# A two-layer hybrid model on one core: the order, one sum and one turning around the half-wide chunk of the gated FFN

## The chip, the cores and the metric

The kernel runs on one core of one Trainium2 chip. The metric is the device time of one execution in microseconds, as the median of several runs. All numbers are float32; the matrix products take float32 values split into a high part in the "fp32r" format and a low part.

## The reference, cut to what matters

Two layers, each with an FFN, a mixer, a cross attention and a second FFN. The change lies in the FFN, which is called four times. `x` is 256 tokens by 1024, the hidden width `D_FF` is 2816.

```python
def swiglu(x, w_gate, w_up, w_down):
    return (jax.nn.silu(x @ w_gate) * (x @ w_up)) @ w_down
...
for l in range(DEPTH):
    h = layer_norm(ALPHA * h + 0.5 * swiglu(h, ffn1_gate[l], ffn1_up[l], ffn1_down[l]),
                   ln_g[l, 0], ln_b[l, 0])
    ...
    h = layer_norm(ALPHA * h + 0.5 * swiglu(h, ffn2_gate[l], ffn2_up[l], ffn2_down[l]),
                   ln_g[l, 3], ln_b[l, 3])
```

## The kernel before

**Products in three parts.** Every weight tile is loaded by a DMA into a `raw` buffer and split (`split`, L74): ScalarE casts it to the high part `whi` (L75), VectorE subtracts that from it for the low part `wlo` (L76). `mm_rows` (L153) then issues three products on TensorE for each pair: high by high, high by low, low by high. All matrix products pass line L129. There are six `raw` buffers and eight of each half, of 128 by 1024 (`bufs` at L86, L106, L107).

**Chunks of the hidden width.** `ffn` (L420) goes through 2816 hidden columns in five chunks of 512 and one, the sixth, of 256, the half-wide chunk. For each it makes the gate's and the up projection's products, applies `silu` and the multiplication, turns the result so that hidden columns lie on partitions (`turn`, L464: four DMAs into the tile `dealt`, two VectorE transposes into `square`, a split into `ah` and `al`), and later multiplies it with two slabs of the down projection (`slab` L732, `both` L756), which add up in four banks called `dn`. Slab (c, u) is the half u of chunk c.

**Chunks by seven.** Some chunks (`sevens`, L738) are computed by `by_seven` (L595), with seven block products for a 2 by 2 block product in place of eight: tokens are halved (tile 0 and 1), the inner width is halved, and gate and up take the place of the two column blocks. The weight sums that this needs are made in place, in the raw tiles: `w00` begins as the gate's first half, `w01` as the up projection's first half, `w10` as the gate's second half, `w11` as the up projection's second half. `parts_of(r, plus)` (L628) first adds `plus` to `r` by VectorE (L632) where it is given, and then splits `r`. `more` (L666) adds a block of a matrix to a raw tile by an adding transfer, a DMA that GpSimd issues (L668). The sums of the tokens' blocks, `bx`, are made once per FFN and held in `kTh` and `kTl`. A `run` (L645) is twelve products into one bank of `o`; `taken` (L663) copies a bank into a tile by ScalarE (L664), and `put` (L650) combines a bank with a tile by VectorE (L651). `o[0]` is used by four runs, of which the second to the fourth go on adding to what the first left: between them `taken` copies the bank's state into `s`, `e` and `f`. For the half-wide chunk those tiles are parts of one called `both`.

In the first FFN of the first layer chunks 2 and 4 go by seven (counted from 0). In the three others chunks 2, 4 and 5 do, so the half-wide chunk 5 is computed by seven three times.

**The order around the half-wide chunk.** In the program's order it runs: `o[0]` with `w00`; `o[1]` with `bx[0]` and `w00` plus `w01`; `o[2]` with `w10`; the first half of the products of slab (3,0) (`between[0]`, the list given at L774, half of them because `steps` is `(0,)`); `o[0]` with `bx[1]` and `w00` plus `w11`; then, since `steps` at L690 is reversed for this chunk, `o[3]` with `bx[3]` and `w11`; `o[0]` with `bx[2]` and `w01`; `o[0]` with `part_of_x(1, 1)` and `w00` plus `w10`. `left` (L695) then does the activation, the multiplication (L698) and the turning. Behind that come the other half of slab (3,0), slab (3,1), and in `ending` (L806) slabs (4,0), (4,1) and (5,0).

**What sets the order of execution.** The program is not executed in the order in which it is written. Within each engine a scheduler of the framework, when the program is built, sets the order: it runs its own estimate of every instruction and takes, whenever an engine is free, the first instruction in the program's order that it believes ready. On the chip each engine then works in that fixed order and waits by semaphores. `tc.issue_after(ins)` queues what its block emits for the engine of `ins` behind `ins`; instructions for other engines are not held. `lows[-1]` is the last emitted VectorE subtraction of a split. The DMA issues stand in the queues of SyncE (SP), ScalarE and GpSimd (POOL).

Of the kernel before, what the change touches and what calls it, by code (L numbers as in the profile page):

```python
# [8 lines left out]
F32 = mybir.dt.float32  # L9
# [8 lines left out]
P = 128  # L18
# [4 lines left out]
NT = SEQ // P  # L23
# [5 lines left out]
CHUNK = 512  # L29
# [31 lines left out]
def model(ctx: ExitStack, tc: tile.TileContext, t: dict, out: bass.AP):  # L61
    nc = tc.nc
# [9 lines left out]
    loads, normed, lows, turns = [], [], [], []  # L72

    def split(hi, lo, src):  # L74
        nc.scalar.copy(hi, src)  # L75
        lows.append(nc.vector.tensor_tensor(lo, src, hi.bitcast(F32), op=ALU.subtract))  # L76
# [343 lines left out]
    def ffn(l, name, n, pend=None, last=False, early=None):  # L420
        gate, up, down = (t[f"{name}_{x}"][l] for x in ("gate", "up", "down"))
        with tc.tile_pool(name="ffn", bufs=2, reuse_waits="tile") as fp:
            acts = []

            def act_tiles():
                ah = fp.tile([P, 4, SEQ], F32R, tag="ah", name="ah", bufs=3)
                al = fp.tile([P, 4, SEQ], F32R, tag="al", name="al", bufs=3)
                return ah, al
# [33 lines left out]


            def turn(s):  # L464
                ah, al = act_tiles()
                n = s.shape[2] // P
                x = fp.tile([P, 4, NT, P], F32, tag="dealt", name="dealt", bufs=1)[:, :, :, 0 : 32 * n]
                for a in range(4):
                    (nc.scalar if n < 4 and a % 2 else nc.sync).dma_start(x[a * 32 : a * 32 + 32], s[:, :, a * 32 * n : (a + 1) * 32 * n])
                d = fp.tile([P, NT, 4, P], F32, tag="up", name="square", bufs=1)[:, :, 0:n, :]  # L470
                for i in range(NT):
                    nc.vector.transpose(
                        d[:, i].rearrange("p k (b r) -> p b k r", b=4),
                        x[:, :, i, :].rearrange("p b (k j) -> p b k j", k=n),
                    )
                d = d.rearrange("p i k t -> p k i t")
                split(*(y[:, 0:n].rearrange("p k (i t) -> p k i t", i=NT) for y in (ah, al)), d)
                return ah, al

            def first():  # L480

# [113 lines left out]
            def by_seven(c0, ncol, bx, between):  # L595
# [76 lines left out]
                taken(s[:, 0, :], o[0])  # L672
                run(o[1], bx[0], parts_of(w00, w01))
                more(w01, up, 1)
                run(o[2], part_of_x(0, 1), parts_of(w10))
                between[0]()
                put(s[:, 0, :], o[2], ALU.add, s[:, 0, :])
                w11 = block(up, 1, pieces(*homes[2]))
                run(o[0], bx[1], parts_of(w00, w11), True)
                if ncol == CHUNK:  # L680
                    more(w00, gate, 1)
                taken(e, o[0])
# [4 lines left out]
                    lambda: (run(o[0], bx[2], parts_of(w01), True), taken(f, o[0])),  # L687
                    lambda: (o.append(bank()), run(o[3], bx[3], parts_of(w11))),
                ]
                for step in steps if ncol == CHUNK else steps[::-1]:  # L690
                    step()
                put(f, o[1], ALU.subtract, f)
                run(o[0], part_of_x(1, 1), parts_of(w00, None if ncol == CHUNK else w10), True)
# [46 lines left out]
            bx = []  # L740
# [24 lines left out]
            later = (0, 0, 0, 2, 0, 2) if early is None else (0, 1, 0, 1, 0, 2)  # L765
            for c, (c0, ncol) in enumerate(chunks):
                if not c:
                    acts.append(first())
                    ys = [[acc((P, 512), "dn") for _ in range(2)] for _ in range(NT)]
                elif c in sevens:  # L770
                    half = []
                    left = by_seven(
                        c0, ncol, bx,
                        [lambda: both(*todo.pop(0))] * 2 if ncol == CHUNK else  # L774
                        [lambda: (half.append(slab(3, 0)), both(3, 0, half[0], (0,))), lambda: None],
                    )
                else:
                    acts.append(hidden(c0) if ncol == CHUNK else last_hidden(c0, turn_memory))
                if c == 1 and early is None:
                    bx.extend(blocks_of_x())  # L780
                if c == 5:
# [8 lines left out]
                    nc.gpsimd.tensor_copy(early_memory[:, 0:2048:256], acts[2][0][:, 0, 0:8].bitcast(F32))  # L790
                    turn_memory = load_memory(fp, loads[-1])
                if c in sevens:
                    acts.append(left())
                    if ncol < CHUNK:
                        both(3, 0, half[0], (1,))
                        both(3, 1)
                else:
                    for _ in range(later[c]):
                        both(*todo.pop(0))
# [539 lines left out]
```

## Time and profile before

| | us |
|---|---|
| median of 3 runs | 1067.16 |
| lowest and highest | 1066.97, 1067.39 |
| the profiled execution | 1066.68 |
| its span, first to last instruction | 1065.0 |
| TensorE busy within the span | 1052.1 |
| VectorE busy within the span | 933.6 |
| ScalarE busy within the span | 661.5 |

The granted TensorE clock of the profiled execution is 0.998 of full speed. The profile is that of one execution. PE is TensorE, DVE VectorE, ACT ScalarE, POOL GpSimd and SP SyncE; L129 is line 129 of the kernel. A row of the timeline gives the start in us from the span's start, the duration, engine, line and operation, output and inputs, the number of instructions merged, and in brackets the engine's idle time before it and what ended that. A matrix product's duration in the timeline is longer than its distance to the next, since they overlap; the distance is what it costs.

### The profile page before, as it was taken

The page shows a single profiled execution, that of the slowest core. Times are in us where ns is not written, and L with a number is a line of the kernel's source. Part 1 is how long each engine was busy: PE and PEld are TensorE (multiplying, and loading weights), DVE is VectorE, ACT ScalarE, POOL GpSimd, SP SyncE. Part 2 cuts the span into 40 slices and gives each one's busy share as a digit, 9 for nine tenths or more (in the row PEclk, how much of TensorE's full clock was granted, in tenths as well). Part 3 has the DMA queues.
Part 4 walks back from the last instruction along what each step waited for, and adds up shares of the span by engine and source line. Part 5 has one row for each costly group of instructions (what it writes and reads, how often), then busy time and mean ns, then how long its engine had stood idle before and what let it go on. Part 6 is the DMA issues. An engine that isn't in the chain of part 4 may idle for free.

```text
span 1065.0 us, 16506 instructions
## 1 busy us (share of the span) xinstructions
PE 1052.1 (99%) x6014; PEld 934.7 (88%) x6014; DVE 933.6 (88%) x1246; ACT 661.5 (62%) x909; POOL 90.9 (9%) x122
## 2 busy tenths in 40 slices
PE   9999999999999999999999999999999999999997
PEld 7888888989899888889888888888998998888886
DVE  6998898989988789888998987989899788898787
ACT  6675775676557466655665755666774655675661
POOL 8002001000000001010001001010000000000000
PEclk9999999999999999999999999999999999999999
DMA  9999984754675589987788987866636665899862
GB/s 363 294 310 289 261 273 158 250 168 153 215 270 183 166 279 234 356 193 223 246 298 232 315 259 208 270 219 223 204 118 221 238 232 176 240 300 298 236 185 76
DMA packets 143745, 251.06 MB, mean 236 GB/s; under 512 B 12784, under 2 KB 53520, under 8 KB 143664
## 3 DMA queue, kind: packets, MB, share of 16 engines
q1 hardware_dynamic: 130656, 228.89, 64.1%
q0 software_dynamic: 10800, 19.55, 10.7%
q10 hardware_dynamic: 2208, 1.57, 0.5%
q8 instruction: 47, 0.77, 0.3%
q14 instruction: 34, 0.28, 0.1%
HBM read 234.50 MB, written 1.05 MB: 221 GB/s over the span
## 4 chain that ended last, share of the span: by engine, by line
PE 92%; DVE 4%; ACT 2%; issue 1%; DMA 1%; ACTq 0%; DVEq 0%
PE acc L129 60%; PE dn L129 29%; DVE wlo L76 2%; ACT whi L75 1%; PE acc L196 1%; DVE raw L632 1%; PE dn L1024 0%; DMA lng<-in_ln_g_dram 0%; DMA h<-in_x_dram 0%; DVE halves L651 0%; PE dn L1098 0%; DVE sg L698 0%; PE acc L512 0%; PE dn L1097 0%; PE dn L1086 0%
## 5 line engine op out<-in xcount | busy, mean ns | idle before, releaser
L75 ACT CAST whi<-raw 128x1024 fp32r<-128x1024 f32 (+1 forms) x453 | 456.4, 1042 | 202.6 <-PE dn L129 60.9
L76 DVE TENSOR_TENSOR wlo<-raw,whi 128x1024 fp32r<-128x1024 f32 (+1 forms) x453 | 534.2, 1208 | 52.5 <-ACT whi L75 47.9
L129 PE MATMUL acc<-whi,xT 128*128 128x512 f32 (+1 forms) x1064 | 314.0, 373 | 3.4 <-ACT both L664 3.4
L129 PEld LDWEIGHTS acc<-whi,xT 128*128 128x128 f32 x1064 | 199.1, 189 | 31.2 <-ACT both L664 4.6
L129 PE MATMUL acc<-wlo,xT 128*128 128x512 f32 (+1 forms) x532 | 197.9, 372 | 0.0
L129 PE MATMUL dn<-whi,ah 128*128 128x512 f32 x346 | 131.5, 380 | 0.0
L129 PE MATMUL dn<-wlo,ah 128*128 128x512 f32 x346 | 131.1, 379 | 0.0
L129 PE MATMUL dn<-whi,al 128*128 128x512 f32 x346 | 131.1, 379 | 0.0
L129 PE MATMUL acc<-xT,whi 128*128 128x512 f32 x480 | 117.8, 382 | 0.2
L129 PEld LDWEIGHTS acc<-wlo,xT 128*128 128x128 f32 x532 | 100.6, 189 | 13.2
L129 PEld LDWEIGHTS acc<-xT,whi 128*128 128x128 f32 x480 | 86.6, 190 | 10.5 <-ACT whi L75 0.7
L129 PE MATMUL dn<-whi,xT 128*128 128x512 f32 x288 | 87.8, 381 | 0.0
L129 PEld LDWEIGHTS dn<-whi,al 128*128 128x128 f32 x346 | 65.4, 189 | 9.3
L129 PEld LDWEIGHTS dn<-whi,ah 128*128 128x128 f32 x346 | 65.4, 189 | 9.0
L129 PEld LDWEIGHTS dn<-wlo,ah 128*128 128x128 f32 x346 | 65.4, 189 | 8.9
L129 PEld LDWEIGHTS acc<-xT,wlo 128*128 128x128 f32 x480 | 62.9, 191 | 3.2
L129 PE MATMUL acc<-xT,wlo 128*128 128x256 f32 x480 | 63.3, 275 | 0.0
L129 PE MATMUL acc<-wlo,kTh 128*128 128x512 f32 (+1 forms) x176 | 61.7, 351 | 0.0
L129 PE MATMUL acc<-whi,kTl 128*128 128x512 f32 (+1 forms) x176 | 61.7, 351 | 0.0
L129 PE MATMUL acc<-whi,kTh 128*128 128x512 f32 (+1 forms) x176 | 61.7, 351 | 0.0
L129 PEld LDWEIGHTS dn<-whi,xT 128*128 128x128 f32 x288 | 54.4, 189 | 7.6 <-DVE xT L76 0.2
L129 PE MATMUL dn<-wlo,xT 128*128 128x512 f32 x144 | 54.6, 379 | 0.0
(245 smaller groups left out, 1288.6 us busy)
## 6 DMA issues: line engine op xcount, KB each, us to landing
raw<-in_ffn_up_dram SPq DMA_DIRECT2D x88, 512.0 KB, 5.7
raw<-in_ffn_down_dram SPq DMA_DIRECT2D x88, 512.0 KB, 6.1
raw<-in_ffn_gate_dram SPq DMA_DIRECT2D x84, 512.0 KB, 5.4
raw<-in_w_in_dram SPq DMA_DIRECT2D x48, 512.0 KB, 4.8
dealt<-sg SPq DMA_DIRECT2D x80, 128.0 KB, 4.9
raw<-in_ffn_up_dram POOLq DMA_DIRECT2D x19, 512.0 KB, 6.0
raw<-in_ffn_gate_dram POOLq DMA_DIRECT2D x16, 512.0 KB, 10.1
raw<-in_ca_k_dram SPq DMA_DIRECT2D x16, 512.0 KB, 5.3
```

What stands on the lines that cost most here:

```text
L75: nc.scalar.copy(hi, src)
L76: lows.append(nc.vector.tensor_tensor(lo, src, hi.bitcast(F32), op=ALU.subtract))
L129: nc.tensor.matmul(o, w, x, start=start, stop=stop, skip_group_check=more)
L196: turns.append(nc.tensor.transpose(pt[:, k, :], src[:, (4 * j + k) * P : (4 * j + k + 1) * P], unit))
L632: nc.vector.tensor_tensor(r[i], r[i], plus[i], op=ALU.add)
```

## The change

Three edits, all of which take effect only where chunk 5 goes by seven.

1. The products of the first half of slab (3,0) come after the run of `o[0]` with `bx[1]` (they move from `between[0]` to `between[1]`), and the runs with `bx[2]` and `bx[3]` go in the order in which they are listed, as in the wide chunks. So each of the uses of `o[0]` from the second on has other products ahead of it.
2. `w00`, holding gate's first half plus up's first half at that point, gets up's second half by a second adding transfer. It was added from `w11` by VectorE.
3. `turn` now gives back a function with its second part (the transposes and the split). For chunk 4 that part is emitted after the whole of `by_seven` of chunk 5, with VectorE's share queued behind the last subtraction of it; everywhere else it is called at once.

```diff
--- before.py
+++ after.py
@@ -462,20 +462,25 @@
 
 
             def turn(s):
-                ah, al = act_tiles()
                 n = s.shape[2] // P
                 x = fp.tile([P, 4, NT, P], F32, tag="dealt", name="dealt", bufs=1)[:, :, :, 0 : 32 * n]
                 for a in range(4):
-                    (nc.scalar if n < 4 and a % 2 else nc.sync).dma_start(x[a * 32 : a * 32 + 32], s[:, :, a * 32 * n : (a + 1) * 32 * n])
-                d = fp.tile([P, NT, 4, P], F32, tag="up", name="square", bufs=1)[:, :, 0:n, :]
-                for i in range(NT):
-                    nc.vector.transpose(
-                        d[:, i].rearrange("p k (b r) -> p b k r", b=4),
-                        x[:, :, i, :].rearrange("p b (k j) -> p b k j", k=n),
-                    )
-                d = d.rearrange("p i k t -> p k i t")
-                split(*(y[:, 0:n].rearrange("p k (i t) -> p k i t", i=NT) for y in (ah, al)), d)
-                return ah, al
+                    queue = nc.scalar if n < 4 and a % 2 else nc.sync
+                    queue.dma_start(x[a * 32 : a * 32 + 32], s[:, :, a * 32 * n : (a + 1) * 32 * n])
+
+                def rest():
+                    ah, al = act_tiles()
+                    d = fp.tile([P, NT, 4, P], F32, tag="up", name="square", bufs=1)[:, :, 0:n, :]
+                    for i in range(NT):
+                        nc.vector.transpose(
+                            d[:, i].rearrange("p k (b r) -> p b k r", b=4),
+                            x[:, :, i, :].rearrange("p b (k j) -> p b k j", k=n),
+                        )
+                    d = d.rearrange("p i k t -> p k i t")
+                    split(*(y[:, 0:n].rearrange("p k (i t) -> p k i t", i=NT) for y in (ah, al)), d)
+                    return ah, al
+
+                return rest
 
             def first():
 
@@ -672,11 +677,13 @@
                 taken(s[:, 0, :], o[0])
                 run(o[1], bx[0], parts_of(w00, w01))
                 more(w01, up, 1)
+                if ncol < CHUNK:
+                    more(w00, up, 1)
                 run(o[2], part_of_x(0, 1), parts_of(w10))
                 between[0]()
                 put(s[:, 0, :], o[2], ALU.add, s[:, 0, :])
                 w11 = block(up, 1, pieces(*homes[2]))
-                run(o[0], bx[1], parts_of(w00, w11), True)
+                run(o[0], bx[1], parts_of(w00, w11 if ncol == CHUNK else None), True)
                 if ncol == CHUNK:
                     more(w00, gate, 1)
                 taken(e, o[0])
@@ -687,7 +694,7 @@
                     lambda: (run(o[0], bx[2], parts_of(w01), True), taken(f, o[0])),
                     lambda: (o.append(bank()), run(o[3], bx[3], parts_of(w11))),
                 ]
-                for step in steps if ncol == CHUNK else steps[::-1]:
+                for step in steps:
                     step()
                 put(f, o[1], ALU.subtract, f)
                 run(o[0], part_of_x(1, 1), parts_of(w00, None if ncol == CHUNK else w10), True)
@@ -765,17 +772,17 @@
             later = (0, 0, 0, 2, 0, 2) if early is None else (0, 1, 0, 1, 0, 2)
             for c, (c0, ncol) in enumerate(chunks):
                 if not c:
-                    acts.append(first())
+                    acts.append(first()())
                     ys = [[acc((P, 512), "dn") for _ in range(2)] for _ in range(NT)]
                 elif c in sevens:
                     half = []
                     left = by_seven(
                         c0, ncol, bx,
                         [lambda: both(*todo.pop(0))] * 2 if ncol == CHUNK else
-                        [lambda: (half.append(slab(3, 0)), both(3, 0, half[0], (0,))), lambda: None],
+                        [lambda: None, lambda: (half.append(slab(3, 0)), both(3, 0, half[0], (0,)))],
                     )
                 else:
-                    acts.append(hidden(c0) if ncol == CHUNK else last_hidden(c0, turn_memory))
+                    acts.append(hidden(c0)() if ncol == CHUNK else last_hidden(c0, turn_memory))
                 if c == 1 and early is None:
                     bx.extend(blocks_of_x())
                 if c == 5:
@@ -790,7 +797,10 @@
                     nc.gpsimd.tensor_copy(early_memory[:, 0:2048:256], acts[2][0][:, 0, 0:8].bitcast(F32))
                     turn_memory = load_memory(fp, loads[-1])
                 if c in sevens:
-                    acts.append(left())
+                    if ncol < CHUNK:
+                        with tc.issue_after(lows[-1].ins):
+                            acts[4] = acts[4]()
+                    acts.append(left() if c + 1 in sevens else left()())
                     if ncol < CHUNK:
                         both(3, 0, half[0], (1,))
                         both(3, 1)
```

## The prediction

> **What bounds the kernel now.** I read the page first: where the span lies, and how much of it each engine works.
>
> ```profile
> span 1065.0 us, 16506 instructions
> ...
> PE 1052.1 (99%) x6014; PEld 934.7 (88%) x6014; DVE 933.6 (88%) x1246; ACT 661.5 (62%) x909; POOL 90.9 (9%) x122
> ```
>
> TensorE (PE) works 1052.1 of 1065.0 us. The change adds and removes no matrix product, so it can gain only what PE stands idle, and it loses whatever new idle time it makes. The view of waits, for PE alone, has three rows:
>
> ```profile
> PE acc L129 <- ACT both L664: 3.4, 3, 1.2
> PE dn L493 <- DVE kTh L488: 1.5, 1, 1.5
> PE acc L512 <- DMA h<-in_x_dram: 0.6, 1, 0.6
> ```
>
> The last two are the start of the kernel, which the diff doesn't touch. The first is the target: three waits, 3.4 us together, 1.12 us each, for a copy of the tile `both` by `taken` (L664). Only the half-wide chunk has that tile, and three of the four FFN calls run that chunk by seven. So **3.4 us is all that can be won**. The timeline of PE shows the first of the three places. A "dn" row is a product of the down projection, "xT" and "kTh" are the chunk's own.
>
> ```profile
> 497.72 0.28 PE L129 MATMUL acc<-whi,xT 128*128 128x256 f32 x1
> ...
> 499.06 0.38 PE L129 MATMUL dn<-whi,ah 128*128 128x512 f32 x1
> ...
> 501.66 0.27 PE L129 MATMUL acc<-whi,kTh 128*128 128x256 f32 x1
> ...
> 502.99 0.28 PE L129 MATMUL acc<-whi,kTh 128*128 128x256 f32 x1
> ...
> 504.33 0.28 PE L129 MATMUL acc<-whi,kTh 128*128 128x256 f32 x1
> ...
> 505.67 0.38 PE L129 MATMUL dn<-whi,ah 128*128 128x512 f32 x1
> ...
> 506.75 0.38 PE L129 MATMUL dn<-whi,al 128*128 128x512 f32 x1
> 508.30 0.38 PE L129 MATMUL acc<-whi,xT 128*128 128x256 f32 x1 [1.17 <-ACT both L664]
> ```
>
> A run of 12 half-wide products takes 499.06 - 497.72 = 1.34 us, a dn product (506.75 - 505.67) / 5 = 0.216 us. The order is: the run into `o[2]`; 12 dn products (2.6 us); `o[0]` with `bx[1]` at 501.66; `o[3]`; `o[0]` with `bx[2]` at 504.33; six dn products that the program emits later; a gap; the last run into `o[0]`. That run may not start before `taken(f, o[0])` has read the bank, and ScalarE (ACT) did so late:
>
> ```profile
> 499.24 1.99 ACT L75 CAST whi<-raw 128x1024 fp32r<-128x1024 f32 x2 [2.29 <-DVE raw L632]
> ...
> 505.04 2.94 ACT L75 CAST whi<-raw 128x1024 fp32r<-128x1024 f32 x3 [1.48 <-DVE raw L632]
> 507.89 0.36 ACT L664 COPY both<-acc 128x256 f32<-128x256 f32 x1
> ```
>
> The bank's last product started just before 505.67; the copy stood behind three casts and ran at 507.89.
>
> **The change part by part.**
>
> *Other products between uses of the bank.* The 12 dn products of slab (3,0) move from before the `bx[1]` run to behind it, and `bx[2]` and `bx[3]` run in the program's order. Then 2.6 us of dn products cover `taken(e)`, and the run into `o[3]`, 1.34 us, covers `taken(f)`. That copy needs 0.36 us and two handovers of some 0.1 us; with one cast of 1.04 us ahead of it 1.6 us, which would leave 0.3 us idle; behind three casts again, the 1.12 us of before. Before, the only cover was the six dn products, 1.3 us; now the 1.34 us stand in the program's order and dn products can still be added to them, while the cast of the last run's weights, first of the three, comes no earlier. So I take nothing, and keep 0 to 1.12 for the range. Credit: 1.12 us a chunk.
>
> *The third sum by an adding transfer.* One VectorE (DVE) addition goes (L632, `w00` plus `w11`). In its place GpSimd (POOL) issues a second adding transfer (L668) behind that into `w01`. It may start only when the split of `w00` plus `w01` has read the tile, and the split of the third sum, for the `bx[1]` run, now waits for its landing.
>
> ```profile
> 488.64 1.23 DVE L632 TENSOR_TENSOR raw<-raw 128x1024 f32<-128x1024 f32 x1
> 491.06 1.23 DVE L76 TENSOR_TENSOR wlo<-raw,whi 128x1024 fp32r<-128x1024 f32 x1 [1.19 <-ACT whi L75]
> ...
> 497.94 1.22 DVE L632 TENSOR_TENSOR raw<-raw 128x1024 f32<-128x1024 f32 x1
> ...
> 500.32 3.50 DVE L76 TENSOR_TENSOR wlo<-raw,whi 128x1024 fp32r<-128x1024 f32 x3 [0.56 <-ACT whi L75]
> ```
>
> ```profile
> 490.18 1.29 POOL L668 DMA_DIRECT2D raw<-in_ffn_up_dram  x1 [16.24 <-DMA lnb<-in_ln_b_dram]
> ```
>
> The rows of DVE, and below them the one of POOL, give the start. The addition of 488.64 ends at 489.87, and the transfer that reads its result is issued at 490.18, 0.31 later. The split of 491.06 ends at 492.29, so the new one is issued at **492.60**; POOL is free by then (490.18 + 1.29). PE ends its run into `o[2]` at 499.06, 6.46 us later. The second and third chunk have the same distance, to a tenth: their splits end at 660.17 and 1017.97, their `o[2]` runs at 667.03 and 1024.83.
>
> ```profile
> 658.95 1.22 DVE L76 TENSOR_TENSOR wlo<-raw,whi 128x1024 fp32r<-128x1024 f32 x1 [1.19 <-ACT whi L75]
> ```
>
> ```profile
> 1016.75 1.22 DVE L76 TENSOR_TENSOR wlo<-raw,whi 128x1024 fp32r<-128x1024 f32 x1 [1.19 <-ACT whi L75]
> ```
>
> ```profile
> 667.03 0.38 PE L129 MATMUL dn<-whi,ah 128*128 128x512 f32 x1
> ```
>
> ```profile
> 1024.83 0.38 PE L129 MATMUL dn<-whi,ah 128*128 128x512 f32 x1
> ```
>
> How long an adding transfer of this size takes stands in the view of line L668: over the whole run with those who waited for it, then alone for 453 to 458 (two issues 2.4 us apart) and 471 to 475 (two, 1.1 us apart). Last, the traffic of 492 to 496, where the one into `w01` is nearly alone.
>
> ```profile
>   ACT whi L75: 13.2, 8
> ...
> DMA to landing us min/median/max: 5.6/6.7/12.4
> ```
>
> ```profile
> DMA to landing us min/median/max: 5.8/6.2/6.7
> ```
>
> ```profile
> DMA to landing us min/median/max: 5.7/9.1/12.4
> ```
>
> ```profile
> q0 software_dynamic: 528, 0.52, 88.4%
> ```
>
> One such transfer fills 88% of all DMA engines for 4 us, so two of them follow one another rather than overlap. With the median, 6.7 us, the new one lands at 499.30, 0.24 us after PE has ended `o[2]`. Then comes the split:
>
> ```profile
> L75 ACT CAST whi<-raw 128x1024 fp32r<-128x1024 f32 (+1 forms) x453 | 456.4, 1042 | 202.6 <-PE dn L129 60.9
> L76 DVE TENSOR_TENSOR wlo<-raw,whi 128x1024 fp32r<-128x1024 f32 (+1 forms) x453 | 534.2, 1208 | 52.5 <-ACT whi L75 47.9
> ```
>
> 1.04 for the cast, 1.21 for the low part, 0.2 of handovers: both halves are there 0.24 + 2.45 = 2.7 us after the end of `o[2]`. Only the first product (0.11 us) does without the low part, so PE would wait **2.6 us** with nothing ahead of the run, 1.5 with the shortest landing (5.6), 8.3 with the longest (12.4). Before, the 12 dn products filled 2.6 us at this very place. The program's order no longer puts them there; the scheduler may, as it did with the six at 505.67, but only for as long as it believes the weights late. The trace says how it judges these transfers: ACT stood eight times, 13.2 us in all, at a cast whose adding transfer had not landed. It takes them 1.65 us too short on average, and a wait that was misjudged isn't filled. So the wait lies between 1.65 (it fills to where it believes) and 2.6 (it fills nothing). No row decides between them; I take the middle, **2.1 us a chunk**.
>
> [...]
>
> What queues behind the wait: on ACT, the casts of `w01` and `w11` and of slab (3,0), unless they are placed ahead of it, all needed after the run that waits; on POOL nothing more in this chunk. The removed addition frees 1.22 us of DVE, but the wait for the landing sits in its place: the old cast was at 499.24, the new one could be at 499.35. So DVE gains PE nothing here. The added traffic (2.6 to 3.4 us of all engines) pushes what SP issues next; below it DVE's rows around the two turnings, and PE's first use of the sixth chunk's:
>
> ```profile
> 495.78 1.46 SPq L97 DMA_DIRECT2D raw<-in_ffn_down_dram  x2
> 498.05 2.67 SPq L469 DMA_DIRECT2D dealt<-sg  x4
> ```
>
> ```profile
> 506.12 1.23 DVE L76 TENSOR_TENSOR wlo<-raw,whi 128x1024 fp32r<-128x1024 f32 x1 [0.30 <-ACT whi L75]
> 507.26 1.30 DVE L472 STREAM_TRANSPOSE square<-dealt 128x512 f32<-128x512 f32 x2
> ...
> 511.05 1.22 DVE L76 TENSOR_TENSOR al<-square,ah 128x1024 fp32r<-128x1024 f32 x1
> ...
> 520.26 0.68 DVE L76 TENSOR_TENSOR al<-square,ah 128x512 fp32r<-128x512 f32 x1
> ```
>
> ```profile
> 521.40 0.38 PE L129 MATMUL dn<-whi,ah 128*128 128x512 f32 x1
> ...
> 521.83 0.38 PE L129 MATMUL dn<-whi,al 128*128 128x512 f32 x1
> ```
>
> The slab that the loads of 495.78 bring was cast at 506.00 and 506.94, in the run of casts at 505.04; so I cost the push at nothing, and at up to 2 us a chunk if the loads and the adding transfer hold each other up.
>
> *The fifth chunk's turning queued later.* Its transposes and split get a place behind the chunk's last low part. They stood there already: that low part ran at 506.12, the transposes at 507.26. SP's and ACT's transfers of `dealt` stay where they were. Their result is complete at 511.05 + 1.22 = 512.27. PE wants it after the last run (508.30 + 1.34 = 509.64) and 30 dn products more, at 516.1, so 3 us of delay would still be covered: nothing. The sixth chunk's turning is closer. Its low half was ready at 520.26 + 0.68 = 520.94 and used at 521.83: if PE comes 1.1 us earlier and DVE doesn't, 0.2 us are lost.
>
> **The sum.** Per chunk -1.12 + 2.1 + 0 + 0 = +1.0; three chunks +3.0 us. The profiled execution took 1066.68 us (span 1065.0 and 1.7 around it): 1069.7. The median of the runs is 0.48 higher, so **1070.2 us**, against 1067.16.
>
> **The rivals**, by the same median.
>
> 1. *The products fill the wait* (faster). The scheduler puts all 12 dn products, or 12 of the 24 of slab (3,0), ahead of the `bx[1]` run. Then it starts at 501.66 as now, the weights are there at 501.75, and the 1.12 us go: 1067.16 - 3.4 = 1063.8. It decides from 10 products on (2.1 us). For it: the six it moved at 505.67. Against it: the 13.2 us by which it misjudged these landings.
> 2. *Half filled.* Five to nine products ahead leave 0.7 to 1.5 us idle, about what goes: 1066 to 1068.5.
> 3. *The transfers collide.* The new one shares the engines with the loads of 495.78 as the pair of 471 to 475 did, and lands at 9 to 10 us instead of 6.7: +2.6 us a chunk more, 1076 to 1080. Against it: the pair of 453 to 458, issued 2.4 us apart as here, landed after 5.8 and 6.7.
> 4. *The transfer is short*. If it lands within 4.1 us, by 496.7, the weights are split when PE ends `o[2]` (496.7 + 2.45 - 0.11 = 499.04): no wait, 1063.8. Against it stands the shortest landing of this line, 5.6. [...]
>
> **How the numbers follow.** About 0.2% (2.1 us, 0.7 a chunk) is what a measurement of this kernel tells from no change. Chances: forecast 0.42 (1069.3 to 1074); first rival 0.31; second 0.18; third 0.06; fourth 0.03. Faster is the first and fourth, 0.34; within 0.2% the second, 0.18; slower the forecast and the third, 0.48. Both signs carry weight, so the range runs from 1063.7 to 1074.0 and leaves out the third rival and the edges; the forecast's own range is 1069.3 to 1074.0.
>
> **What would show it.** In the view of PE's waits the row "ACT both L664" should be gone or under 0.5 us. In its place should stand waits of the `acc<-whi,kTh` products on `whi` (ACT L75) or `wlo` (DVE L76), three times some 2 us, and ACT's casts should wait for POOL L668 three times more. DVE should show three additions fewer on L632, POOL three transfers more on L668. If no PE wait follows the `o[2]` runs and dn rows stand there instead, rival 1 is right. The forecast is wrong if the new transfer lands within 4 us, or if PE's time falls by more than 3.4 us, which no row here could explain.

## The result, and the profile after

The changed kernel takes **1083.93 us** (median of five runs, 1082.73 to 1084.33) against 1066.97 for the kernel before (five runs, 1066.27 to 1067.39). The ratio is 1.0156, its 95% interval 1.0142 to 1.0171: slower by 17.0 us, where the forecast was slower by 3.0. The profiled execution took 1082.95 us, 16.3 more than that of before.

The page of the changed kernel, its first rows. Line numbers have moved: `taken` is now L669, `put` L656, the addition in `parts_of` L637, the adding transfer L673.

```profile
span 1081.2 us, 16492 instructions
...
PE 1060.3 (98%) x6014; PEld 940.3 (87%) x6014; DVE 929.7 (86%) x1243; ACT 662.9 (61%) x909; POOL 94.7 (9%) x125
```

The edit did what it says: VectorE has three instructions fewer and GpSimd three more. TensorE has the same 6014 products, and yet it is busy 8.2 us longer, besides standing idle 8 us longer. So two things have to be found: idle time, and products that became slower. The waits of PE in the changed kernel (us in total, times, longest):

```profile
PE acc L129 <- ACT both L669: 8.5, 3, 3.5
PE acc L196 <- DVE h L378: 3.3, 2, 1.6
PE dn L498 <- DVE kTh L493: 1.5, 1, 1.5
PE acc L517 <- DMA h<-in_x_dram: 0.5, 1, 0.5
```

The first row looks like the old wait grown from 3.4 to 8.5 us. It is another one: it stands ahead of another run, and behind another copy. The second row is new. I follow the first chunk from the cause on.

**The transfer lands when it was expected to.** The timeline of POOL, and the view of line L673 for 492 to 494 alone, who waited for it and how long it took:

```profile
490.31 1.29 POOL L673 DMA_DIRECT2D raw<-in_ffn_up_dram  x1 [16.16 <-DMA lnb<-in_ln_b_dram]
492.71 1.28 POOL L673 DMA_DIRECT2D raw<-in_ffn_up_dram  x1 [1.12 <-DVE wlo L76]
```

```profile
  ACT whi L75: 6.6, 1
...
DMA to landing us min/median/max: 6.4/6.4/6.4
```

Issued at 492.71, landed 6.4 us later at 499.1. The second and third chunk's take 6.3 and 7.3 us. The prediction had 492.60 and 499.30.

**But ACT stood before it from the start.** The timeline of ACT around the landing:

```profile
491.55 1.05 ACT L75 CAST whi<-raw 128x1024 fp32r<-128x1024 f32 x1
499.17 1.04 ACT L75 CAST whi<-raw 128x1024 fp32r<-128x1024 f32 x1 [6.58 <-DMA raw<-in_ffn_up_dram]
500.12 0.59 ACT L454 ACTIVATE sg<-acc 128x512 f32<-128x512 f32 x1
500.61 1.03 ACT L75 CAST whi<-raw 128x1024 fp32r<-128x1024 f32 x1
501.55 0.37 ACT L669 COPY both<-acc 128x256 f32<-128x256 f32 x1
```

The cast of the third sum stands right behind that of `w10`. ACT reaches it at 492.60, and does nothing for 6.58 us. The activation of chunk 4 and the copy of `o[0]` into `s`, which stand behind it, run at 500.12 and 501.55; in the kernel before, which had nothing to wait for there, they ran at 495.25 and 496.58. They were ready here too: the last product of the run into `o[0]` starts at 496.48 and takes 0.28 us. That copy is what frees the bank for the very run that waits. VectorE lives on ACT's casts and stands empty too, for 5.50 us:

```profile
494.07 0.68 DVE L656 TENSOR_TENSOR halves<-acc,halves 128x512 f32<-128x512 f32 x1
500.25 1.22 DVE L76 TENSOR_TENSOR wlo<-raw,whi 128x1024 fp32r<-128x1024 f32 x1 [5.50 <-ACT whi L75]
```

The low part is there at 501.47, but PE has to wait for the copy behind it:

```profile
499.16 0.28 PE L129 MATMUL acc<-whi,xT 128*128 128x256 f32 x1
501.97 0.38 PE L129 MATMUL acc<-whi,kTh 128*128 128x256 f32 x1 [2.54 <-ACT both L669]
502.19 0.28 PE L129 MATMUL acc<-wlo,kTh 128*128 128x256 f32 x1
```

The gaps of the three chunks at this place are 2.54, 2.48 and 3.49 us.

**Behind each gap the clock is lower.** Windows of the changed kernel: stretch, length, busy time (and instructions) of PE, PEld, DVE, ACT and POOL, granted clock, DMA share, GB/s.

```profile
498.00:502.00 4.00, 1.46 (x14) 1.27 (x13) 1.75 (x2) 2.83 (x5) 0.00 (x0) 1.00 0.16 25
502.00:506.00 4.00, 4.00 (x17) 3.70 (x18) 4.00 (x5) 3.45 (x5) 0.00 (x0) 0.57 0.37 103
506.00:510.00 4.00, 4.00 (x31) 3.79 (x29) 2.95 (x4) 0.96 (x2) 0.00 (x0) 1.00 1.00 254
...
676.00:680.00 4.00, 4.00 (x16) 3.44 (x16) 4.00 (x6) 2.86 (x5) 0.00 (x0) 0.57 0.36 104
...
1039.50:1045.00 5.50, 5.50 (x19) 4.96 (x20) 5.50 (x7) 3.50 (x5) 0.00 (x0) 0.50 0.59 125
```

In 502 to 506 PE is busy throughout and starts 17 products, in the next four microseconds 31. A mean clock of 0.57, with half the clock as in the last row, means 3.4 of 4.0 us at half. The two stretches mix wide and half-width products differently, but the half-width ones alone show it too: they come every 0.21 us from 502.47 on and every 0.11 us from 507.65 on. The third chunk, after the longest gap, has 5.5 us of work at half the clock. With products twice as far apart, 0.21 for 0.11 us, a busy stretch at half the clock does half its work. That gives an estimate of 1.7 + 1.7 + 2.75 = 6.2 us of work lost. That is most of the 8.2 us by which PE is busy longer.

**The new wait at the norm.** VectorE in the changed kernel, at the end of the first FFN with such a chunk, and under it the kernel before at the same place:

```profile
529.84 0.21 DVE L362 TENSOR_SCALAR mv<-st 128x1 f32<-128x1 f32 x1
531.80 0.69 DVE L352 SCALAR_TENSOR_TENSOR h<-h,dn 128x512 f32<-128x512 f32 x1 [1.75 <-PE dn L129]
532.41 0.08 DVE L352 DVE_READ_ACCUMULATOR h<-h,dn 128x1 f32 x1
532.41 0.15 DVE L366 TENSOR_SCALAR rs<-mv 128x1 f32<-128x1 f32 x1
```

```profile
526.45 0.15 DVE L366 TENSOR_SCALAR rs<-mv 128x1 f32<-128x1 f32 x1 [1.31 <-ACT kTh L365]
```

In the kernel before `rs` of the first token tile comes first, and the second tile's update of `h` (L352) follows when PE has its sums. In the changed kernel that update stands ahead of `rs`, and waits 1.75 us for PE, while PE's next products wait for what `rs` leads to. It is the order that the scheduler chose, 25 us behind the edit.

**The account.** The spans differ by 1081.2 - 1065.0 = 16.2 us. The waits give 8.5 + 3.3 - 3.4 = 8.4, the clock 6.2: 14.6. The remaining 1.6 us lie in time that counts as busy: behind the waits the products stand further apart. The eight at the norm (L196), for example, take 1.23 us in the first FFN with such a chunk, 0.87 before.

One thing doesn't fit the clock's share. Four of the five executions have a mean granted clock of 0.993 or 0.994; the fifth has 0.996, and at 1084.33 us it is no shorter. No trace of it was kept, so how far the 6.2 us hold for every execution stays open.

### The profile page after: what moved, and what is told of

Its sections match the earlier page's. It is cut to its first block, busy times and chain, and to the rows that moved or that the text cites. A ratio compares the mean times of both kernels' runs of the same rounds, so it can differ in the third digit from the quotient of the medians.

```text
span 1081.2 us, 16492 instructions
## 1 busy us (share of the span) xinstructions
PE 1060.3 (98%) x6014; PEld 940.3 (87%) x6014; DVE 929.7 (86%) x1243; ACT 662.9 (61%) x909; POOL 94.7 (9%) x125
## 4 chain that ended last, share of the span: by engine, by line
PE 93%; DMA 3%; DVE 2%; ACT 1%; issue 1%; ACTq 0%; DVEq 0%
PE acc L129 61%; PE dn L129 29%; DMA raw<-in_ffn_up_dram 2%; PE acc L196 1%; ACT whi L75 1%; DVE wlo L76 1%; DMA lng<-in_ln_g_dram 1%; PE dn L1034 0%; DVE raw L637 0%; PE dn L1108 0%; DMA h<-in_x_dram 0%; PE acc L517 0%; DVE h L378 0%; DVE h L373 0%; PE dn L1107 0%
## 5 line engine op out<-in xcount | busy, mean ns | idle before, releaser
L673 POOL DMA_DIRECT2D raw<-in_ffn_up_dram x22 | 26.9, 1222 | 316.4 <-DVE raw L637 131.4
```

What stands on the lines that cost most here:

```text
L673: nc.gpsimd.dma_start(x, part_of(m, j, i), accum_op=ALU.add)
```

## The experiments

The theory (A in the texts on record) was that the landing of the adding transfer makes the loss, through ACT's place in front of it and the clock. The rivals B to D put it elsewhere: on the new order, on the turning, or on something else than the landing. Each experiment's time stands beside runs of the kernel before on the same chip.

### The edits one by one

**The order alone:** the first edit, with the sum on VectorE as before and the turning as before.

```diff
-                for step in steps if ncol == CHUNK else steps[::-1]:
+                for step in steps:
...
-                        [lambda: (half.append(slab(3, 0)), both(3, 0, half[0], (0,))), lambda: None],
+                        [lambda: None, lambda: (half.append(slab(3, 0)), both(3, 0, half[0], (0,)))],
```

> Only the first edit: slab (3,0)'s products between the second and third use of the bank, bx[2] and bx[3] in the listed order; the third sum stays with VectorE. Theory A (the loss comes from the adding transfer: its landing holds ScalarE's queue, PE stands idle for it and the clock falls): no loss here, the three waits of 1.1 us shrink, 1063.5 to 1067. Rival B (the order is what costs: the run with bx[1] has lost the 2.6 us of products ahead of it, and VectorE's addition is late for it too): PE waits 1 to 2.5 us at each of the three places, 1068 to 1075.

1071.9 us against 1067.28; 1.0043 (1.0028 to 1.0058), so 4.6 us slower. The waits of PE:

```profile
PE acc L196 <- DVE h L378: 3.3, 2, 1.6
PE acc L129 <- ACT both L664: 3.1, 3, 1.0
```

Neither side had this right: A expected no loss, B a wait of 1 to 2.5 us at each of the three places. The new order brings the wait at the norm by itself, and the old wait, which it was meant to remove, stays: 3.1 us for 3.4. The copy into `f` now stands behind the cast for the last run, and that cast waits for VectorE's addition. The mean granted clock is 0.999.

**The transfer alone:** the second edit, with the order of before, in which 12 down products stand ahead of the run that waits.

```diff
+                if ncol < CHUNK:
+                    more(w00, up, 1)
...
-                run(o[0], bx[1], parts_of(w00, w11), True)
+                run(o[0], bx[1], parts_of(w00, w11 if ncol == CHUNK else None), True)
```

> Only the second edit: the third sum by the adding transfer, slab (3,0)'s products at their old place ahead of it, bx[3] before bx[2]. Theory A: landing still near 6.5 us after the issue, ScalarE still held; the 2.6 us of products cover most of it, PE waits 0 to 1 us at the bx[1] run, too short for the clock to fall; the old waits may stay: 1066 to 1071. Rival B (the transfer is harmless, the order costs): 1066 to 1068 with the old three waits and no other.

1083.52 us; 1.0150 (1.0135 to 1.0165), 16.2 us slower, as much as the whole change. The expected size was far too small. The waits of PE, and the timeline of ACT around the largest of the first chunk:

```profile
PE acc L129 <- ACT both L664: 11.3, 4, 3.5
```

```profile
506.56 1.99 ACT L75 CAST whi<-raw 128x1024 fp32r<-128x1024 f32 x2 [1.91 <-DVE raw L632]
508.45 0.36 ACT L664 COPY both<-acc 128x256 f32<-128x256 f32 x1
```

```profile
508.87 0.44 PE L129 MATMUL acc<-whi,kTh 128*128 128x256 f32 x1 [3.46 <-ACT both L664]
```

The down products do hide the landing itself: ahead of the `bx[1]` run PE stands 0.11 us. What they don't hide comes one use of the bank later. ACT and VectorE have lost 4.85 and 3.39 us of lead at the landing, the copy into `e` comes behind two casts that wait for a late addition, and the `bx[2]` run waits 3.46 us for it. The mean granted clock is 0.991, against 0.998 before. So the cost isn't that nothing stood ahead of the run. (The parts don't add up, either: 4.6 and 16.2 us are more than the 17.0 of the whole change.)

**The turning alone:** the third edit.

```diff
+                    if ncol < CHUNK:
+                        with tc.issue_after(lows[-1].ins):
+                            acts[4] = acts[4]()
+                    acts.append(left() if c + 1 in sevens else left()())
```

> Only the third edit: the fifth chunk's transposes and split queued behind the last low part of the sixth. Theory A: nothing, 1066 to 1068, the three waits of 1.1 us as before. Rival C (this edit reorders VectorE's queue up to the layer norm, and the two new waits of 1.64 us for h at the end of the second and third FFN come from it): 1069 to 1071, with these two waits in PE's view.

1067.05 us in ten runs; 0.9994 (0.9985 to 1.0004). No effect, and the old waits as they were. **Order and turning,** that is, the changed kernel with the third sum back on VectorE:

```diff
-                if ncol < CHUNK:
-                    more(w00, up, 1)
...
-                run(o[0], bx[1], parts_of(w00, w11 if ncol == CHUNK else None), True)
+                run(o[0], bx[1], parts_of(w00, w11), True)
```

> The first and third edit without the second: the changed kernel with the third sum made by VectorE. Theory A: 1063.5 to 1067, no clock below 1.0, no wait for a landing. Rival B: 1068 to 1080, most of the loss stays. Rival C: the two waits for h alone, 1067 to 1070.

1072.08 us; 1.0042 (1.0028 to 1.0056), with the same two rows of waits as the order alone (3.3 at the norm, 3.1 for `both`). The turning adds nothing to that either. A's range, up to 1067, was missed, and the loss is only a part of what B meant: the order's own cost of 4.6 to 4.8 us was in neither.

### What the landing costs

**The third sum left out:** the changed kernel with neither transfer nor addition (the up projection's second half is missing from that sum).

```diff
-                if ncol < CHUNK:
-                    more(w00, up, 1)
```

> The changed kernel with the third addition left out altogether: no adding transfer into w00 and no VectorE addition, so the bx[1] products of the sixth chunk lack the up projection's second half; everything else as changed. Theory A (the wait for the landing of that transfer, on ScalarE, is the loss): the waits of 2.5 to 3.5 us, the half clock and the empty ScalarE stretch of 6.6 us go; what is left is what the order alone made, 1067 to 1072. Rival D (the order of ScalarE's queue that the scheduler writes is the loss, whether the data is late or not): PE still waits 2 us or more at the bx[1] runs, 1076 or more.

1069.51 us against 1066.89; 1.0026 (1.0014 to 1.0037), 2.6 us slower. So 17.0 - 2.6 = 14.4 us of the loss hang on the transfer. The clock is 0.998, the norm has no wait, and PE's wait for `both` is 4.6 us in five places. So the transfer makes most of the loss, as the theory has it. This run doesn't tell its landing from its traffic; the next one does in part.

**The split queued later:** the changed kernel, with the cast of the third sum behind the copy into `s` on ACT. The transfer, its landing and PE's order stay.

```diff
-                taken(s[:, 0, :], o[0])
+                kept_s = taken(s[:, 0, :], o[0])
...
-                run(o[0], bx[1], parts_of(w00, w11 if ncol == CHUNK else None), True)
+                with tc.issue_after(kept_s.ins) if ncol < CHUNK else nullcontext():
+                    third = parts_of(w00, w11 if ncol == CHUNK else None)
+                run(o[0], bx[1], third, True)
```

> The changed kernel; the third sum's cast is queued on ScalarE behind the copy of o[0] into s (L669), so that the copy, the activation and the casts of slab (3,0) no longer stand behind it. The transfer and its landing stay. Theory A in its narrow form (PE waits for the data): the wait at the bx[1] run stays at 1.7 to 2.5 us, with ACT whi or DVE wlo as its end instead of ACT both, and 3 to 8 us come back because ScalarE and VectorE work through the landing: 1075 to 1081. Rival E (PE waits only for the copy into s, which stood behind the cast): the wait is under 1 us, 1070 to 1075. Rival D: no change, 1082 to 1085.

1078.64 us; 1.0112 (1.0099 to 1.0126). Its loss is 11.75 us, so the cast's place in ACT's queue made 17.0 - 11.75 = 5.2 us. The waits of PE, and ACT in the first chunk:

```profile
PE acc L129 <- ACT whi L75: 5.3, 5, 2.2
PE acc L129 <- DVE wlo L76: 2.6, 3, 0.9
PE acc L196 <- DVE h L378: 1.8, 2, 0.9
```

```profile
496.57 0.37 ACT L669 COPY both<-acc 128x256 f32<-128x256 f32 x1 [0.79 <-PE acc L129]
499.43 4.83 ACT L75 CAST whi<-raw 128x1024 fp32r<-128x1024 f32 x5 [2.49 <-DMA raw<-in_ffn_up_dram]
```

Here the copy is out of the way at 496.57, and PE waits for the data alone: 1.37 + 0.88 = 2.25 us in the first chunk, 1.26 + 0.88 = 2.14 in the second, 2.16 + 0.88 = 3.04 in the third. This is the wait that the prediction took at 2.1. Together it is 1.1 us less than the three gaps of the changed kernel (2.54, 2.48, 3.49): the copy held up the run itself by little, since the data came late too. More came back at the norm, whose wait fell from 3.3 to 1.8 us, and by the clock, whose mean is 0.996 against 0.993: it stays at full in the first chunk and falls in the third. The two chunks, in pieces of 3.41 us (as long as each of the first two stretches at half in the changed kernel):

```profile
497.64:501.05 3.41, 1.89 (x15) 1.51 (x13) 0.54 (x1) 1.62 (x2) 0.00 (x0) 1.00 0.77 191
501.05:504.46 3.41, 2.68 (x18) 2.52 (x19) 3.41 (x5) 3.41 (x6) 0.00 (x0) 1.00 0.14 37
...
1030.08:1033.49 3.41, 1.25 (x9) 0.88 (x8) 0.39 (x1) 1.46 (x2) 0.00 (x0) 1.00 0.60 158
1033.49:1036.90 3.41, 2.53 (x13) 2.52 (x13) 3.41 (x5) 3.37 (x4) 0.00 (x0) 0.50 0.11 14
1036.90:1040.31 3.41, 3.41 (x10) 2.69 (x10) 3.41 (x5) 0.69 (x2) 0.00 (x0) 0.50 0.87 293
```

**The wait filled:** the changed kernel with 22 further products of half width ahead of the run that waits. They go to the bank of `o[3]`, before its run begins it anew.

```diff
+                if ncol < CHUNK:
+                    o.append(bank())
+                    with tc.issue_after(made[-1].ins):
+                        for _ in range(22):
+                            nc.tensor.matmul(o[3], xTh[:, 0, 0:P], kTh[:, 0, :], start=True, stop=True)
```

> The changed kernel with 22 products of 128x256 more, into the bank of o[3] before its first use, queued behind the run into o[2]: 2.46 us of work whose result is overwritten, in a wait of 2.5 to 3.5 us. Theory F (the halved clock is a loss of its own, brought on by the idle time): the granted clock stays 1.0 at these places and 1.7 us return at each of the first two, up to 3.4 at the third, 1076 to 1080. Rival G (the clock falls for another reason, or its fall costs nothing): 1083 to 1085, or more by the products' 2.46 us where they don't fit into the wait.

1079.98 us; 1.0123 (1.0109 to 1.0137). PE gets work that is worth nothing, and the kernel becomes 3.9 us faster than the changed one. The clock no longer falls within the work (mean 0.999 against 0.993). The 66 added products alone take 7.4 us, at 1.34 / 12 us each, and yet PE's busy time grows only from 1060.3 to 1061.4: the clock gives back some 6.3 us, as the windows had it. The waits didn't stay as they were, so the 3.9 us aren't the clock's alone. At the norm 2.8 us went (3.3 to 0.5), where VectorE now has `rs` first, as in the kernel before; around the run 1.9 us went (8.5 to 4.4 + 2.2). The bank of `o[3]` was held by the activation, which stood behind the cast, so that the added products waited themselves.

```profile
PE acc L687 <- ACT sg L454: 4.4, 3, 1.6
PE acc L129 <- ACT both L669: 2.2, 3, 0.8
```

### Whether a version beats both kernels

**The copy first, in the kernel before:** the casts of slab (3,1) queued behind the copy into `f`.

```diff
-                        both(3, 1)
+                        with tc.issue_after(copies[-1].ins):
+                            a = slab(3, 1)
+                        both(3, 1, a)
```

> The kernel before with one line of order: ScalarE's casts of slab (3,1) are queued behind the copy of o[0] into f (taken, L664), which stood behind them. Nothing else is changed. If the old waits of 1.1 us came only from that place in the queue, they fall to 0.3 us or less and 2 to 2.6 us are won: 1064.5 to 1065.3. If the last run waits as long for its own weights (low part ready 0.9 us after the casts began) they fall to 0.6: 1065.5 to 1066.5. If the later casts starve slab (3,1)'s products or VectorE's row up to the layer norm, 1067 to 1071.

1067.72 us in eleven runs; 1.0008 (0.9999 to 1.0017). The wait for the copy is gone, and in its place PE waits for low parts of weights, 1.8 us in three places. Nothing is won.

**The order, with the norm's order held:** the order alone, and the second tile's update of `h` queued behind the first tile's norm.

```diff
+                    with tc.issue_after(normed[-1].ins) if pin and i and not last else nullcontext():
                         nc.vector.scalar_tensor_tensor(
```

> The first edit alone (as in e1_order_only), and VectorE's update of h for the second token tile is queued behind the layer norm of the first (after L378), where it stood ahead of that norm's rs. Theory H (the two waits of 1.64 us for h are VectorE's queue: it stood for the second tile's products while the first tile's norm was ready): both go, 3.3 us return, 1068 to 1069. Rival (the norm is late for another reason, such as VectorE being behind): the waits stay near 1.6 us and the time at 1071 to 1073.

1070.67 us against 1067.03; 1.0034 (1.0021 to 1.0048). The waits of PE:

```profile
PE acc L129 <- ACT both L665: 3.1, 3, 1.0
PE acc L196 <- DVE h L379: 1.6, 2, 0.8
```

Half of the norm's wait is gone (3.3 to 1.6 us), and 4.6 us of loss become 3.6. So the order of VectorE at the norm was about half of that wait; what makes the other half stays open. Neither expected range (up to 1069, from 1071) had the time.

**All 12 products ahead of the last run:** the kernel before, with the second half of slab (3,0) written ahead of the last run into `o[0]`, which the scheduler had done with half of them.

```diff
+                if ncol < CHUNK:
+                    between[2]()
```

> The kernel before, with all 12 products of slab (3,0)'s second half written ahead of the last run into o[0], where the scheduler had put six and left a wait of 1.1 us. If the wait is a gap that products fill: the three waits go, 2.5 to 3.4 us are won, 1063.5 to 1064.5. If the layer norm's queue is rearranged as it was by the first edit: two waits of 1.6 us for h come in, 1066 to 1068. If the sixth chunk's turning then comes too late (0.9 us to spare before): 0.2 to 0.5 us a chunk are lost again, 1064.5 to 1066.

1070.49 us; 1.0031 (1.0019 to 1.0043). The old waits are gone, and others stand there:

```profile
PE dn L129 <- ACT ah L75: 3.0, 3, 1.2
PE acc L196 <- DVE h L378: 1.8, 2, 0.9
```

The last run comes later, and with it the sixth chunk's activation and turning; PE needs their result 0.65 to 1.2 us before it is there. All three expected ranges, up to 1068, were missed. **The two together, with the new order:**

```diff
-                for step in steps if ncol == CHUNK else steps[::-1]:
+                for step in steps:
...
+                if ncol < CHUNK:
+                    between[2]()
...
+                    with tc.issue_after(normed[-1].ins) if pin and i and not last else nullcontext():
```

> The first edit, the 12 products of g2 ahead of the last run, and the layer norm's queue of g1; the third sum by VectorE. If the three mechanisms add up: no wait near the half-wide chunk and none for h, 1063.5 to 1065. If VectorE is the bound there once PE doesn't wait (its row is full from 495 to 521): the waits move to wlo, 1066 to 1069.

1070.1 us; 1.0029 (1.0018 to 1.0041), with PE waiting 3.3 us for low parts and 1.6 at the norm. The waits moved to the low parts as expected, but the time lies above both ranges.

**The transfer covered:** the version with the split queued later, and 12 down products ahead of the run again, as in the kernel before.

```diff
-                        [lambda: None, lambda: (half.append(slab(3, 0)), both(3, 0, half[0], (0,)))],
+                        [lambda: (half.append(slab(3, 0)), both(3, 0, half[0], (0,))), lambda: None],
```

> The changed kernel with the third sum's cast queued behind the copy into s (as f2), and slab (3,0)'s first products back ahead of the bx[1] run. The transfer stays. Theory A, and rival 1 of the prediction (2.6 us of products ahead cover the landing): the wait at the bx[1] run falls from 2.25 to 0.5 us or less, the clock stays at 1.0, 1066 to 1070. If the transfer costs beyond its landing (traffic, ScalarE's empty stretch): 1071 to 1077 with waits elsewhere.

1077.15 us (1074.78 to 1079.4); 1.0095 (1.0077 to 1.0113), a miss: with the landing covered and the copy free it should have been near the kernel before. The waits of PE:

```profile
PE acc L129 <- ACT both L669: 4.8, 3, 1.6
PE acc L129 <- DVE wlo L76: 2.5, 3, 1.0
...
PE acc L196 <- DVE h L378: 1.4, 2, 0.7
```

The run still waits 0.7 to 1.0 us, the next one 1.6 us for the copy into `e`, which stands behind a cast that waits for a late addition. In the transfer alone, in the split queued later and here, PE waits for what ACT and VectorE deliver late: an addition of 1.22 us on VectorE, made early, is replaced by a landing for which both stand. The profiled execution is 8.1 us longer than that of before. Of these the waits are 4.8 + 2.5 + 1.4 - 3.4 = 5.3 us and the clock, which falls in the last chunk, 1.5 (its mean is 0.63 from 1037 to 1038 and 0.50 from 1038 to 1040); the rest wasn't separated.

The four executions form two pairs: 1074.78 and 1075.22 us with a mean granted clock of 0.998, 1079.08 and 1079.40 with 0.994 and 0.993. So the same kernel took 4.2 us more in the executions with the lower clock. The trace is of the first; in which chunks the clock of the other pair fell isn't recorded.

No version is faster than the kernel before.

## Why the prediction was wrong

The spans grew by 16.2 us, where the sum has 3.0. Over three chunks the sum has -3.4 and +6.3. In the changed kernel the old waits are gone (-3.4), and the new wait at the `bx[1]` runs is 8.5 us. The other 11.1 us are three things that the sum has at nothing: 6.2 us of work lost at half the clock, 3.3 us of waiting at the norm, 1.6 us of products further apart behind the waits. So the sign and the new wait were right, and two steps failed. The sum per chunk, "-1.12 + 2.1 + 0 + 0", charges PE for a wait with its length alone; this is the larger error. And ACT and VectorE are charged nothing for standing at the landing, which the bullet on the queue below takes up.

- **Only 3.4 us to be won:** not contradicted. Nothing that was run came below the kernel before by more than the noise.
- **The old wait goes (-1.12 a chunk):** wrong in its own edit. With the order alone 1.04 us a chunk remain, since the copy stands behind a cast again, which the prediction had named as a possibility and then not counted. In the changed kernel it is no longer there, but other waits are, and the runs don't show that the order removed it.
- **Issue, landing and split (+2.1 a chunk):** right. Landing at 499.09 against 499.30; with the copy out of the way the wait is 2.25, 2.14 and 3.04 us. The scheduler put no product into it, so the upper bound of 2.6 was nearer than the middle. But the sign that the prediction named, the row "ACT both" gone and waits on `whi` or `wlo` in its place, didn't come: the row grew to 8.5 us, since the copy was there still later than the data.
- **"What queues behind the wait: on ACT, the casts of `w01` and `w11` and of slab (3,0) ..., all needed after the run that waits":** this step failed, and so did "So DVE gains PE nothing here", which took VectorE to lose nothing either. Ahead of the listed casts stood the activation of chunk 4 and the copy into `s`, and that copy is needed by the run that waits. The list was made from the program's order, from what is emitted after the split; the queue of ACT is the scheduler's, which had put the cast 6.6 us ahead of its data. The prediction had the row that says so, 13.2 us of waits at such casts, and used it only to ask whether products would be put ahead. ACT stood 6.58 us at that cast, and the copy behind it, for which PE's products were done at 496.8, ran at 501.55. In the version with the cast queued behind the copy it ran at 496.57; moving this one cast was worth 5.2 us. In the transfer alone, where products cover the landing (PE stands 0.11 us there), ACT still stands 4.85 us and VectorE 3.39, and PE waits 3.46 us a chunk one run later: the lost lead by itself.
- **PE's speed:** not in the sum at all. The prediction took its products at full speed behind every wait. Each gap of 2.5 us was followed by 3.4 us at half the clock, and the longest came with 6.8: 6.2 us by the windows, some 6.3 of PE's busy time when the gap was filled. The kernel before had no such stretch before its last product; its gaps are 1.1 us.
- **The norm:** not in the sum. The wait of 3.3 us comes with the new order alone, but not always: the version without the third sum has the same order and no such wait. It hangs on the scheduler's choice far behind the edit.
- **The removed addition "gains PE nothing":** not quite. Without the sum the norm's wait is gone and the kernel is 2.2 us faster than with the sum on VectorE (2.6 against 4.8 us over before).
- **The turning (0):** right, 0.9994 with its interval around 1.
- **The rivals:** in the third, the collision, the landing of 9 to 10 us didn't come. The first, products that fill the wait, was tried twice by hand, and even so the time was 1.5% and 0.95% above before: covering PE's wait doesn't cover that of ACT and VectorE. The second needed products ahead of the run, and there were none; the fourth needed a landing within 4.1 us, and it took 6.4.
- **The added traffic ("2.6 to 3.4 us of all engines"):** the row beside it, 88.4% of 4 us, gives 3.5. Nothing in the sum hangs on it.

What stays open is why the scheduler believed the transfer so early: its estimate stands in no trace.

## What to carry to other kernels

When a wait is added, read from the profile what stands behind the waiting instruction on its engine in executed order, and ask of each whether the consumer of the awaited data needs it too; the program's order doesn't tell. A transfer that replaces a short addition is not free because it uses an idle queue: here two engines that work just ahead of TensorE lost their lead at its landing, ACT with 6.58 us of standing and VectorE with 5.50. And where TensorE is 99% busy, price a gap by its length and by what the clock does after it: here 3.41 us at half behind a gap of 2.5.

## What the runs showed of the hardware

**TensorE's idle time and the clock.** From where its record begins (6.43 us in the kernel before, 7.39 in the changed one) to the last product, the granted clock in these two profiles is either full or half. The kernel before has no stretch at half there. The changed one has three: from 502.33 to 505.74, from 676.41 to 679.82 and from 1038.22 to 1045.05, so 3.41, 3.41 and 6.83 us. Here are the 3.41 us ahead of each and the stretches themselves, and from 533.05 on the wait at the norm, behind which nothing fell:

```profile
498.92:502.33 3.41, 0.87 (x8) 0.68 (x7) 2.08 (x2) 3.16 (x5) 0.00 (x0) 1.00 0.00 0
502.33:505.74 3.41, 3.41 (x16) 3.14 (x15) 3.41 (x5) 3.12 (x5) 0.00 (x0) 0.50 0.40 113
533.05:536.46 3.41, 1.77 (x13) 1.54 (x13) 3.41 (x6) 2.52 (x4) 0.59 (x1) 1.00 0.03 11
673.00:676.41 3.41, 1.03 (x9) 1.03 (x10) 2.75 (x3) 3.41 (x6) 0.00 (x0) 1.00 0.00 0
676.41:679.82 3.41, 3.41 (x13) 2.87 (x12) 3.41 (x5) 2.45 (x4) 0.00 (x0) 0.50 0.41 120
1034.81:1038.22 3.41, 1.20 (x11) 1.00 (x9) 0.45 (x1) 1.53 (x3) 0.00 (x0) 1.00 0.13 18
1038.22:1041.63 3.41, 2.14 (x10) 2.14 (x11) 3.41 (x4) 3.41 (x6) 0.00 (x0) 0.50 0.05 16
1041.63:1045.05 3.42, 3.42 (x11) 2.88 (x11) 3.42 (x5) 1.37 (x3) 0.00 (x0) 0.50 0.89 186
```

Ahead of the three falls PE stood 2.54, 2.38 and 2.21 of the 3.41 us. In the first two stretches at half it stood no more, and the clock came back at their end. In the third it stood 3.41 - 2.14 = 1.27 us more, and that stretch is twice as long. The two waits of 1.64 us at the norm have no fall behind them, and neither have the three of 1.09 to 1.17 us in the kernel before.

The version with the split queued later has both, in the rows above. In the first chunk its gaps of 1.37 and 0.88 us lie in two pieces (3.41 - 1.89 = 1.5 us idle, then 0.7), and the clock stays at full. In the third chunk the piece from 1030.08 to 1033.49 has 2.16 us idle, and the clock is at half from 1033.49 on. In the covered version PE stood 1.96 of the 3 us from 1034 to 1037, in more than one gap, and the clock fell behind them as well. So what PE waits in a chunk doesn't tell by itself what the clock will cost: 2.25 us in two gaps had no fall behind them in the first chunk, and 2.16 us idle in one piece had one in the third. What decides between gaps of this size, and what sets the times at which the clock falls and comes back, these runs don't show.
